# Reciprocal square roots of a hybrid encoder layer: one GpSimd power instruction in place of eleven VectorE instructions

## The chip, the cores and the metric

The kernel runs on one core of a Trainium2 chip. The metric is the device time in microseconds (us) of one execution. Before the change it is 2738.26 us, the median of three runs (2738.12 to 2742.08). Engines are called by the profile's names: PE (TensorE matmuls), PEld (its weight loads), DVE (VectorE), ACT (ScalarE), POOL (GpSimd) and SP (SyncE, which here issues every DMA).

## What is computed

One layer of an encoder in float32, 2048 tokens by 1024 features:

```
h = rmsnorm(x, norm_mix_w);  proj = h @ w_in
q, k, v, z, xbc, dt_raw, qx = split(proj)
q = partial_rope(rmsnorm(q, q_norm_w));  k = partial_rope(rmsnorm(k, k_norm_w))
attn_out = windowed_gqa(q, k, v, attn_sink)
ssd_out  = bidirectional_ssd(z, xbc, dt_raw, ...)        # its output is gated and rmsnormed in two groups
xatt_out = memory_cross_attention(qx, mem, ...)          # rmsnorm of mem, of its keys and of the queries
x = x + concat(attn_out, ssd_out, xatt_out) @ w_out
x = x + square(relu(rmsnorm(x, norm_mlp_w) @ w_mlp_up)) @ w_mlp_down

rmsnorm(t, w) = t * rsqrt(mean(t * t) + 1e-6) * w
```

Seven norms occur. Each needs, per token (and per head or group), one reciprocal square root: a column of 128 tokens by 2 to 16 numbers at a time.

## The kernel before

Tokens go in tiles of 128, and a tile's tokens lie on the 128 partitions wherever a norm's factors are made. Matmuls in float32 are done as three products of float32r parts: a value is split into a high part (ACT rounds it) and a low part (DVE or POOL subtracts). The program has three stages.

Stage 1 goes over the upper half of the sequence (1024 tokens), then over the lower half. For each half it makes the k, v and dt projection for eight tiles (`kv_products`), the factors of the input norm for the eight tiles at once (`x_stats`, L803), then normalises and rotates k in two groups of four tiles (`kvdt_tiles`, L901, which calls `head_norm`, L666, and `rope`, L691), convolves twelve column blocks (`xbc_col`, L818), and makes the memory queries in pairs of tiles (`xattn_pair`, L1019) and the attention queries in pairs of tiles (`q_pair`, L997). The upper half also makes the memory's keys and values (`mem_kv`, L711). Stage 2 runs the window attention and the state-space part for 16 chunks. Stage 3 makes the output projection for eight pairs of tiles (`out_pair`, L1400) and, one step later, the norm ahead of the MLP (`mid`, L1482); then come the two matmuls of the MLP, in a form with seven block products in place of eight.

Every reciprocal square root is made by `rsqrt` (L497). It is called 40 times: twice in `x_stats` (8 numbers per token), twice in `mem_kv` (2 and 8), four times for k (8), eight times in `xattn_pair` (8), eight times in `q_pair` (16), eight times in `out_pair` (4) and eight times in `mid` (2). Before the change each call is eleven VectorE instructions on at most 128x16 numbers: an integer guess, a scaling, and three Newton steps of three instructions, each of which needs the one before it.

What follows k's factors matters below. In `head_norm` (L666) ACT squares the products scaled by the input norm's factor `r`, DVE sums the squares and adds the epsilon, `rsqrt` follows, DVE multiplies its result by `r` (L673), and POOL multiplies k by that (L677). Then `rope` takes four POOL instructions for each tile (L698 to L701), and PE transposes the tile (`kvdt_tiles`, L919). POOL also makes the low parts of the weights of `xbc_col` (the splits `W<-Z,W`, L481).

The order of the instructions isn't the order in which the code calls them. A recorder (`Program`, L74) collects all of them with their dependences; `plan` (L287) then runs a list schedule over them with a cost in ns for each (`cost`, L176) and a latency between engines (`LAT`, L80), and takes the earliest instruction in program order that is ready on an engine. `schedule` (L399) issues them in that order. So one changed cost moves instructions everywhere behind it, on all engines, and the DMAs on SP with them; each engine then works its own list strictly in order. All of the program's instructions are issued from L414 (L416 after the change), so that tiles, not lines, tell them apart: `small` holds the factors and other small columns, `B` the normalised k and q and the convolution's buffers, `E` the parts of `rope`, `W` and `X` the split weights and inputs of stage 1, `Z` loaded weights, `bank` is PSUM, and `const` holds r (`self.r1`), the identity and the cosines.

Of the kernel before, what the change touches and what calls it, by code (L numbers as in the profile page):

```python
# [10 lines left out]
F32 = mybir.dt.float32  # L11
F32R = mybir.dt.float32r
I32 = mybir.dt.int32
AF = mybir.ActivationFunctionType
ALU = mybir.AluOpType
# [4 lines left out]
P = 128  # L20
# [15 lines left out]
NCOL, NROW = sum(n for _, n in COLS), sum(n for _, n in ROWS)  # L36
# [37 lines left out]
class Program:  # L74
# [101 lines left out]
    def cost(self, eng, name, args, kw, aps):  # L176

        n = max(self.free(args[0] if args else kw["out"]), 1)
        isap = lambda x: isinstance(x, (View, bass.AP))
        if eng == "PE":  # L180
            if name == "transpose":
                return 109
            return 108 if n < 32 else n / 2.4 + 13 if args[1].dtype == F32R and n >= 256 else n * 4 / 2.4 + 6
        if eng == "ACT":
            n_ap = sum(isap(kw.get(k)) for k in ("bias", "scale", "accum_out"))
            return 93 * n_ap + 0.834 * n + (50 if isinstance(args[1], View) and args[1].psum else 93)
        if eng == "DVE":
            if name == "reciprocal":
                return 69 + 6.25 * n
            n = max([n] + [self.free(a) for a in aps])  # L190
            if name == "memset":
                return 9 + 1.04 * n
            ap_scalar = any(isap(x) and self.free(x) == 1 for x in args[2:4]) and "scalar" in name
            fast = name in ("tensor_copy", "tensor_scalar") and not any(isinstance(a, View) and a.psum for a in aps)
            return 69 + (0.52 if fast else 1.041) * n + (61 if ap_scalar else 0)
        if eng == "POOL":
            bcast = any(d[0] == 0 and d[1] > 1 for a in aps[1:] for d in a.ap.ap[1:])
            return 148 + (1.667 if bcast else 2.1) * n if name == "tensor_tensor" else 40 + 1.6 * n
        return 475

# [260 lines left out]
class Hybrid:  # L461
# [34 lines left out]

    def rsqrt(self, pool, v, n):  # L497

        nc = self.nc
        y = pool.tile([P, 32], F32, "nr_y")[:, :n]  # L500
        h = pool.tile([P, 32], F32, "nr_h")[:, :n]
        t = pool.tile([P, 32], F32, "nr_t")[:, :n]
        nc.vector.tensor_scalar(y.bitcast(I32), v.bitcast(I32), -0.5, 1597463007.0, ALU.mult, ALU.add)
        nc.vector.tensor_scalar(h, v, -0.5, None, ALU.mult)
        for _ in range(3):
            nc.vector.tensor_tensor(t, y, y, ALU.mult)
            nc.vector.tensor_tensor(t, t, h, ALU.mult)
            nc.vector.scalar_tensor_tensor(y, t, 1.5, y, ALU.add, ALU.mult)
        return y

    def ps(self):
# [2 lines left out]

    def constants(self):
        nc, a = self.nc, self.a
        sizes = dict(ident=128, ones=128, eps=1, cols=NCOL, r1=16)
        self.mem.use("const", F32, **{"c_" + k: (n, 1) for k, n in sizes.items()})
        sizes = dict(triU=128, triL=128, amask=768, rows=NROW, dt=512, acs=512, wst=512, dec=512, edge=48, negA=32, nsk=8)
        self.mem.use("late", F32, **{"c_" + k: (n, 1) for k, n in sizes.items()})  # L520

        def c(name, shape):
            return self.mem.tile([P] + shape, F32, "c_" + name)

        self.eps = c("eps", [1])
        nc.vector.memset(self.eps, EPS)
        nc.scalar.activation(self.eps, self.eps, AF.Copy)
        self.ident = c("ident", [P])
        make_identity(nc, self.ident)
        self.ones = c("ones", [P])  # L530
        nc.gpsimd.memset(self.ones, 1.0)
        self.triU = c("triU", [P])
        self.triL = c("triL", [P])
        for t, sgn in ((self.triU, 1), (self.triL, -1)):
            nc.gpsimd.affine_select(out=t, in_=self.ones, compare_op=ALU.is_ge, fill=0.0, base=0,
                                    pattern=[[sgn, P]], channel_multiplier=-sgn)
        self.mask = c("amask", [6 * P])
        nc.gpsimd.memset(self.mask, 0.0)
        for o, sgn in ((0, 1), (2, -1), (3, 1), (5, 1)):
            m = self.mask[:, o * P:(o + 1) * P]  # L540
            nc.gpsimd.affine_select(out=m, in_=m, compare_op=ALU.is_ge, fill=NEG, base=0,
                                    pattern=[[sgn, P]], channel_multiplier=-sgn)

        cols, rows = c("cols", [NCOL]), c("rows", [NROW])
        first = NCOL - 256
        self.load(cols[:, :first], a["cols"][:, :first])

        def cut(t, table, name, shape=None):
            at = sum(n for k, n in table[:[k for k, _ in table].index(name)])
            v = t[:, at:at + dict(table)[name]]  # L550
            return v.rearrange("p (a b) -> p a b", a=shape[0]) if shape else v

        self.w_mix, self.w_mem, self.w_mlp, self.w_ssd, self.cb, self.sd = (
            cut(cols, COLS, n) for n in ("w_mix", "w_mem", "w_mlp", "w_ssd", "cb", "sd"))
        self.cw, self.cos, self.sin = cut(cols, COLS, "cw", (NXC,)), cut(cols, COLS, "cos", (NJ,)), cut(cols, COLS, "sin", (NJ,))
        for v in (cut(cols, COLS, "cw"), self.cb):
            nc.vector.tensor_scalar(v, v, 0.5, None, ALU.mult)
        self.qw, self.kw, self.xqw, self.xkw, self.sink, self.dtb, self.al = (
            cut(rows, ROWS, n) for n in ("qw", "kw", "xqw", "xkw", "sink", "dtb", "al"))
        self.r1 = c("r1", [NJ])  # L560
        self.dt = c("dt", [NJ, 32])
        self.acs = c("acs", [NJ, 32])
        self.wst = c("wst", [NJ, 32])
        self.dec = c("dec", [NJ, 32])
        self.edge = c("edge", [NXC, 4])
        self.negA = c("negA", [32])
        self.nsk = c("nsk", [8])
        yield
        self.load(cols[:, first:], a["cols"][:, first:])
        self.load(rows, a["rows"].rearrange("(o n) -> o n", o=1).broadcast_to([P, NROW]))  # L570
        nc.vector.tensor_scalar(self.qw, self.qw, 0.125, None, ALU.mult)
        nc.vector.tensor_tensor(self.xkw, self.xkw, self.xqw, ALU.mult)
        nc.scalar.activation(self.negA, self.al, AF.Exp)
        nc.vector.tensor_scalar(self.negA, self.negA, -1.0, None, ALU.mult)
        nc.vector.tensor_scalar(self.nsk, self.sink, -1.0, None, ALU.mult)
        yield

    def memory(self):
        m = self.mem
        m.use("small", F32, nr_y=(32, 3), nr_h=(32, 3), nr_t=(32, 3), nr_v=(32, 3), xmx=(32, 2), xsm=(32, 2),  # L580
              amx=(32, 3), ang=(32, 3), asm=(32, 3), aes=(32, 3), rm=(32, 1), s2=(32, 2))

    def memory1(self):
# [1181 lines left out]
```

## Time and profile before

| what | value |
|---|---|
| time, median of three runs | 2738.26 us (2738.12 to 2742.08) |
| span of the profiled execution, first to last instruction | 2734.9 us |
| PE busy | 2706.3 us, 99% of the span |
| DVE busy | 1900.8 us, 70%, 3102 instructions |
| ACT busy | 1331.6 us, 49% |
| POOL busy | 554.2 us, 20%, 488 instructions |
| mean granted TensorE clock | 0.997 |

The profile gives the profiled execution's span, which is 3.4 us under the median of the three runs; a start and an end outside the first and last instruction lie around it. Times in the profile are counted from the span's start. A row of a timeline gives start, duration, engine, operation, tiles and shape (rows with xN are N instructions in a row on that engine), and in brackets the idle time of the engine ahead of it with what ended it. `PEclk` is the clock that TensorE was granted, in tenths (or as a share, in the view by windows).

### The profile page before, as it was taken

To read this page: it belongs to the slowest core of one execution; us is meant where nothing else is said; L and a number is where in the kernel's file an instruction comes from. 1 tells how busy PE (TensorE), PEld (TensorE's weight loads), DVE (VectorE), ACT (ScalarE), POOL (GpSimd) and SP (SyncE) were. 2 spreads that over 40 slices of the span, in tenths; PEclk is the share of its full clock that TensorE was granted. 3 is DMA by queue.
4 is the path that set the end of the run, shared out by engine and by line. 5 is a ranking of instruction groups with operands and counts; after the bars stand their busy time and mean duration, and the time that the engine had idled before them with its cause. 6 is when DMAs were issued, how large, how long until landed. Compare 5 with 4: busy or idle time off the path is not lost.

```text
span 2734.9 us, 37074 instructions
## 1 busy us (share of the span) xinstructions
PE 2706.3 (99%) x13486; PEld 2236.3 (82%) x13486; DVE 1900.8 (70%) x3102; ACT 1331.6 (49%) x2229; POOL 554.2 (20%) x488
## 2 busy tenths in 40 slices
PE   8999999999999999999999999999999999999999
PEld 7788887787778888788888888888888888888887
DVE  6884689956677686776666785857757584857666
ACT  6545534353567676733333543535353443535352
POOL 3203444455445554410101000000000000000000
PEclk9999999999999999999999999999999999999999
DMA  6651446545877786865555954536272745435241
GB/s 239 213 182 59 133 147 190 172 158 177 268 251 235 214 257 205 271 204 200 193 192 202 342 195 146 170 102 214 80 259 93 253 162 169 154 119 197 90 165 62
DMA packets 264886, 501.40 MB, mean 183 GB/s; under 512 B 26096, under 2 KB 99072, under 8 KB 264704
## 3 DMA queue, kind: packets, MB, share of 16 engines
q1 hardware_dynamic: 264704, 499.04, 55.3%
q8 instruction: 106, 1.74, 0.3%
q14 instruction: 76, 0.62, 0.1%
HBM read 381.51 MB, written 117.45 MB: 182 GB/s over the span
## 4 chain that ended last, share of the span: by engine, by line
PE 92%; DVE 2%; POOL 2%; ACT 1%; issue 1%; DMA 1%; SPq 0%; DVEq 0%; ACTq 0%; POOLq 0%
PE bank L414 92%; POOL B L414 1%; DVE B L414 1%; DVE A L414 1%; POOL E L414 1%; DVE small L414 0%; DMA Z<-in_w_out_dram 0%; ACT C L414 0%; SPq L414 0%; DMA W<-erow_d 0%; DVE W L414 0%; ACT A L414 0%; ACT B L414 0%; POOL W L414 0%; DVE X L414 0%
## 5 line engine op out<-in xcount | busy, mean ns | idle before, releaser
L414 PE MATMUL bank<-X,late 128*128 128x512 f32 x1792 | 552.3, 389 | 0.0
L414 PE MATMUL bank<-A,E 128*128 128x512 f32 (+2 forms) x1152 | 404.8, 380 | 1.1 <-ACT A L414 0.7
L414 PE MATMUL bank<-X,A 128*128 128x512 f32 (+1 forms) x1264 | 396.1, 390 | 0.2 <-DMA A<-v_d 0.2
L414 PEld LDWEIGHTS bank<-X,late 128*128 128x128 f32 x1792 | 336.3, 188 | 69.6
L414 PE MATMUL bank<-late,C 128*128 128x512 f32 x896 | 348.6, 389 | 0.0
L414 PE MATMUL bank<-late,E 128*128 128x512 f32 x896 | 348.6, 389 | 0.0
L414 PE MATMUL bank<-W,X 128*128 128x512 f32 (+1 forms) x1536 | 339.4, 373 | 6.5 <-ACT W L414 5.8
L414 PE MATMUL bank<-X,W 128*128 128x512 f32 x1344 | 324.3, 398 | 0.7 <-ACT E L414 0.6
L414 PE MATMUL bank<-X,X 128*128 128x512 f32 x1216 | 317.6, 401 | 0.6 <-DVE X L414 0.6
L414 PEld LDWEIGHTS bank<-W,X 128*128 128x128 f32 x1536 | 265.8, 190 | 51.5 <-ACT W L414 5.8
L414 PEld LDWEIGHTS bank<-X,W 128*128 128x128 f32 x1344 | 250.8, 189 | 55.8 <-issue 3.4
L414 PEld LDWEIGHTS bank<-X,X 128*128 128x128 f32 x1216 | 225.2, 188 | 56.0 <-issue 8.9
L414 PEld LDWEIGHTS bank<-A,E 128*128 128x128 f32 x1152 | 211.7, 188 | 43.0 <-issue 2.8
L414 PEld LDWEIGHTS bank<-X,A 128*128 128x128 f32 (+1 forms) x1264 | 192.5, 173 | 50.5 <-issue 3.5
L414 DVE TENSOR_TENSOR A<-Z,late 128x1024 fp32r<-128x1024 f32 x100 | 121.9, 1221 | 149.0 <-ACT late L414 142.6
L414 DVE TENSOR_TENSOR B<-B,bank 128x512 f32<-128x512 f32 x286 | 189.7, 680 | 33.3 <-PE bank L414 32.6
L414 PEld LDWEIGHTS bank<-late,E 128*128 128x128 f32 x896 | 168.2, 188 | 34.9
L414 PEld LDWEIGHTS bank<-late,C 128*128 128x128 f32 x896 | 168.2, 188 | 34.8
L414 ACT CAST late<-Z 128x1024 fp32r<-128x1024 f32 x100 | 105.1, 1051 | 140.0 <-PE bank L414 101.3
L414 ACT ACTIVATE C<-C,small 128x384 f32<-128x384 f32 (+1 forms) x256 | 143.8, 598 | 36.0 <-DVE small L414 35.9
L414 ACT ACTIVATE W<-W 128x512 f32<-128x512 f32 x224 | 134.4, 627 | 48.9 <-DVE W L414 45.9
L414 DVE SCALAR_TENSOR_TENSOR B<-B,const 128x1022 f32<-128x1022 f32 (+1 forms) x96 | 146.0, 1524 | 3.9 <-ACT B L414 3.0
(178 smaller groups left out, 4259.3 us busy)
## 6 DMA issues: line engine op xcount, KB each, us to landing
X<-xc_d SPq DMA_DIRECT2D x112, 1024.0 KB
xc_d<-E SPq DMA_DIRECT2D x56, 512.0 KB
Z<-in_w_z_dram SPq DMA_DIRECT2D x32, 512.0 KB
W<-erow_d SPq DMA_DIRECT2D x64, 256.0 KB
X<-in_w_up_dram SPq DMA_DIRECT2D x32, 512.0 KB
A<-in_w_up_dram SPq DMA_DIRECT2D x32, 512.0 KB
X<-in_w_down_dram SPq DMA_DIRECT2D x32, 512.0 KB
A<-in_w_down_dram SPq DMA_DIRECT2D x32, 512.0 KB
```

What stands on the lines that cost most here:

```text
L414: o.fn(*[fix(x) for x in o.args], **{k: fix(x) for k, x in o.kw.items()})
```

## The change

`rsqrt` becomes one POOL instruction, `tensor_tensor` with the operation power: the variance to the power of a tile that holds -0.5. That tile, `root`, is filled once at the start. The planner gets a cost for such an instruction, 500 ns and 40 ns for each number of a row, so 820 ns for 8 numbers. The buffers of the Newton steps fall away.

```diff
@@ cost
             bcast = any(d[0] == 0 and d[1] > 1 for a in aps[1:] for d in a.ap.ap[1:])
+            if ALU.pow in args:
+                return 500 + 40 * n
             return 148 + (1.667 if bcast else 2.1) * n if name == "tensor_tensor" else 40 + 1.6 * n
@@ rsqrt
-        nc = self.nc
         y = pool.tile([P, 32], F32, "nr_y")[:, :n]
-        h = pool.tile([P, 32], F32, "nr_h")[:, :n]
-        t = pool.tile([P, 32], F32, "nr_t")[:, :n]
-        nc.vector.tensor_scalar(y.bitcast(I32), v.bitcast(I32), -0.5, 1597463007.0, ALU.mult, ALU.add)
-        nc.vector.tensor_scalar(h, v, -0.5, None, ALU.mult)
-        for _ in range(3):
-            nc.vector.tensor_tensor(t, y, y, ALU.mult)
-            nc.vector.tensor_tensor(t, t, h, ALU.mult)
-            nc.vector.scalar_tensor_tensor(y, t, 1.5, y, ALU.add, ALU.mult)
+        self.nc.gpsimd.tensor_tensor(y, v, self.root[:, :n], ALU.pow)
         return y
@@ constants
-        sizes = dict(ident=128, ones=128, eps=1, cols=NCOL, r1=16)
+        sizes = dict(ident=128, ones=128, eps=1, root=32, cols=NCOL, r1=16)
...
+        self.root = c("root", [32])
+        nc.gpsimd.memset(self.root, -0.5)
@@ memory
-        m.use("small", F32, nr_y=(32, 3), nr_h=(32, 3), nr_t=(32, 3), nr_v=(32, 3), xmx=(32, 2), xsm=(32, 2),
+        m.use("small", F32, nr_y=(32, 3), nr_v=(32, 3), xmx=(32, 2), xsm=(32, 2),
```

The planner writes another order for every engine. Three lists at one place, the first normalised k (`kvdt_tiles` for the first four tiles of the upper half, soon after the start), show how. On VectorE, before, from the sum of k's squares on (`TENSOR_REDUCE small`); `late<-E` is the sum of dt and its bias, `B 128x256` belongs to `dt_half`:

```order
L414 TENSOR_REDUCE small_87<-B_101 128x8
L414 TENSOR_SCALAR small_87<-small_87 128x8 x3
L414 TENSOR_TENSOR late_89<-E_103,late_89 128x32
L414 TENSOR_TENSOR small_87<-small_87 128x8
L414 TENSOR_TENSOR late_89<-E_103,late_89 128x32 x2
L414 TENSOR_TENSOR small_87<-small_87 128x8
L414 TENSOR_TENSOR late_89<-E_103,late_89 128x32
L414 SCALAR_TENSOR_TENSOR small_87<-small_87 128x8
L414 TENSOR_TENSOR small_87<-small_87 128x8 x2
L414 SCALAR_TENSOR_TENSOR small_87<-small_87 128x8
L414 TENSOR_TENSOR small_87<-small_87 128x8
L414 TENSOR_SCALAR B_101<-B_101 128x256
```

The same place on VectorE after the change; `small_87<-small_87,const_88` is the product of the factors with r (L673 before):

```order
L416 TENSOR_REDUCE small_87<-B_101 128x8
L416 TENSOR_SCALAR small_87<-small_87 128x8
L416 TENSOR_TENSOR small_87<-small_87,const_88 128x8
L416 TENSOR_TENSOR late_89<-E_103,late_89 128x32 x4
L416 TENSOR_TENSOR B_101<-bank_77,Z_102 128x512
```

The Newton instructions are gone, and the product with r stands right behind the epsilon. On GpSimd, before, from the weight splits on; `B_101<-B_101,small_87` multiplies k by its factors, and the rows with `E_103` are `rope`:

```order
L414 TENSOR_TENSOR W_0_98<-Z_102,W_0_97 128x1024 x4
L414 TENSOR_TENSOR B_101<-B_101,small_87 128x512
L414 TENSOR_TENSOR E_103<-B_101,const_88 128x32 x2
L414 TENSOR_TENSOR B_101<-E_103 128x2x8
L414 TENSOR_TENSOR E_103<-B_101,const_88 128x32
L414 TENSOR_TENSOR B_101<-E_103 128x2x8
```

And after, where `small_87<-const_88` is the power of `x_stats` and `small_87<-small_87,const_88` the power for k:

```order
L416 TENSOR_TENSOR W_0_98<-Z_102,W_0_97 128x1024
L416 TENSOR_TENSOR small_87<-const_88 128x8
L416 TENSOR_TENSOR small_87<-small_87,const_88 128x8
L416 TENSOR_TENSOR W_0_98<-Z_102,W_0_97 128x1024 x2
L416 TENSOR_TENSOR B_101<-B_101,small_87 128x512
L416 TENSOR_TENSOR E_103<-B_101,const_88 128x32 x3
L416 TENSOR_TENSOR B_101<-E_103 128x2x8
```

Two splits now stand behind the power for k and ahead of the product with k, and one split (of four) has gone behind the rotations. On PE, before, around the first transpose of a k tile (`const_88,B_101`; the others are products of `xbc_col`):

```order
L414 MATMUL bank_77<-X_0_93,W_0_98 128x512
L414 MATMUL bank_80<-X_0_93,W_0_98 128x512
L414 MATMUL bank_77<-X_0_93,W_0_97 128x512
L414 MATMUL bank_78<-const_88,B_101 128x128
L414 MATMUL bank_77<-X_0_94,W_0_97 128x512
```

And after the change:

```order
L416 MATMUL bank_79<-X_0_94,W_0_97 128x512
L416 MATMUL bank_77<-const_88,B_101 128x128
L416 MATMUL bank_79<-X_0_93,W_0_98 128x512
L416 MATMUL bank_79<-X_0_93,W_0_97 128x512
L416 MATMUL bank_77<-const_88,B_101 128x128
```

Before, 55 products of `xbc_col` stand between the last product of `kv_products` and this transpose; after the change 26 do, and the four transposes of the group stand within 13 places, where before they were spread over 47. The transpose of r by `x_stats` (`bank<-const 8x128`) has moved seven products forward. The four k groups, the query pairs and stages 2 and 3 are reordered too; the number of PE instructions is the same.

## The prediction

> **What bounds the kernel now.** I read the page first: busy times and the granted clock in 40 slices.
>
> ```profile
> span 2734.9 us, 37074 instructions
> PE 2706.3 (99%) x13486; PEld 2236.3 (82%) x13486; DVE 1900.8 (70%) x3102; ACT 1331.6 (49%) x2229; POOL 554.2 (20%) x488
> PEclk9999999999999999999999999999999999999999
> ```
>
> PE is busy for 2706.3 of 2734.9 us, so it is the bound, and 28.6 us is all that lies between its instructions. VectorE, which the change relieves, is at 70%. Next I looked at where PE idles, by stretches, and then at who ends its waits (columns: us in total, times, longest).
>
> ```profile
> 1175.00:1525.00 350.00, 350.00 (x1628) 291.48 (x1627) 230.32 (x489) 124.62 (x193) 40.78 (x56) 1.00 0.59 207
> 1525.00:2735.00 1210.00, 1206.33 (x5329) 998.91 (x5327) 812.84 (x850) 539.26 (x686) 0.00 (x0) 1.00 0.48 161
> ```
>
> The first row is the output projection, where 16 of the 40 square roots are: PE has no idle time there at all. The second is the MLP, without square roots; its 3.7 us of idle is the end of the program. So whatever the change can bring must come from stages 1 and 2.
>
> ```profile
> PE bank L414 <- POOL B L414: 8.1, 7, 3.3
> PE bank L414 <- ACT W L414: 5.8, 1, 5.8
> ```
>
> The second is the start of the program (the first weights). The first is the one that matters: POOL's tile `B` is a normalised and rotated k or q that PE is to transpose, so behind each of these seven waits stands a square root. I then went to each. The two long ones are the first two groups of k, A and B below; these are PE's rows there.
>
> ```profile
> 45.36 12.67 PE L414 MATMUL bank<-X,W 128*128 128x512 f32 x55
> 61.38 0.33 PE L414 MATMUL bank<-const,B 128*128 128x128 f32 x1 [3.35 <-POOL B L414]
> ...
> 85.72 6.86 PE L414 MATMUL bank<-X,W 128*128 128x512 f32 x29
> 94.71 0.33 PE L414 MATMUL bank<-const,B 128*128 128x128 f32 x1 [2.13 <-POOL B L414]
> ```
>
> A costs 3.35 us of waiting and B 2.13 us. Each has a second price, which the windows show (PE busy and count, granted clock, DMA share, GB/s):
>
> ```profile
> 62.00:65.40 3.40, 3.40 (x9) 0.50 0.00 0
> 65.40:80.00 14.60, 14.60 (x70) 1.00 0.57 158
> 96.00:99.50 3.50, 3.50 (x13) 0.52 0.48 150
> 731.00:737.80 6.80, 5.98 (x32) 0.50 0.98 315
> ```
>
> Behind each of these two waits the clock is granted at half for 3.4 us, which takes up to 1.7 us more of PE's time. A is thus worth 5.05 us and B 3.83 us. (The third dip, at 731 us, is at the start of stage 2, where no square root is.) The other waits for square roots are small: from 320 to 362 us, the first of the lower half, and from 660 to 685 us, the last queries.
>
> ```profile
> PE bank L414 <- POOL B L414: 1.1, 2, 0.8
> PE bank L414 <- ACT E L414: 0.6, 1, 0.6
> PE bank L414 <- DVE A L414: 0.3, 1, 0.3
> ...
> PE bank L414 <- POOL B L414: 1.5, 3, 0.7
> ```
>
> That is C, 2.0 us, and D, 1.5 us. All that a perfect square root could give back is 5.05 + 3.83 + 2.0 + 1.5 = 12.4 us, 0.45% of the time. A measurement of this kernel can tell about 0.2%, 5.5 us, from no change.
>
> **What is removed.** 40 calls of eleven instructions are 440: 240 products, 120 fused ones, 80 with a scalar. Their groups (count | busy, mean ns):
>
> ```profile
> L414 DVE TENSOR_TENSOR small<-small 128x8 f32<-128x8 f32 (+3 forms) x273 | 61.3, 224 | 15.5 <-ACT C L414 10.2 <-ACT small L414 0.3
> L414 DVE SCALAR_TENSOR_TENSOR small<-small 128x2 f32<-128x2 f32 (+3 forms) x152 | 36.3, 242 | 3.6
> L414 DVE TENSOR_SCALAR small<-small 128x8 f32<-128x8 f32 (+7 forms) x106 | 21.6, 235 | 5.4 <-ACT B L414 4.3
> ```
>
> 240 x 0.224 + 120 x 0.242 + 80 x 0.235 = 102 us of VectorE. On the time that is worth nothing by itself: VectorE isn't the bound, and PE's work hides it. What counts is the latency of a call where PE waits, and how the new order uses it.
>
> **What is added.** 40 power instructions on POOL. The trace of before has none, so I bound one by POOL's shortest and longest group with two inputs:
>
> ```profile
> L414 POOL TENSOR_TENSOR B<-E 128x16 f32<-128x16 f32 x32 | 10.4, 339 | 0.5
> L414 POOL TENSOR_TENSOR W<-Z,W 128x1024 fp32r<-128x1024 f32 x38 | 96.0, 2530 | 204.1 <-ACT W L414 201.9 <-PE bank L414 2.2
> ```
>
> It is not below 0.34 us, the price of a 128x16 subtraction, and I take 2.53 us as the other end. A power of 2 to 16 numbers is nearer to the small row; I take the planner's own 0.82 us for 8 numbers, which lies in between and by which the order was made. For all 40 that is about 33 us of POOL, which is at 20%. A rule of the Trainium skill speaks against the move: GPSIMD Engine Reference, section 4.1, calls GpSimd the wrong engine for elementwise work, about twice as slow as VectorE for two inputs. The rows agree (339 ns for a small POOL instruction, 224 ns for a small one of VectorE, its stalls included). By that rule alone a power would cost 0.34 us instead of 0.82, and A below would be 0.5 us better; but eleven instructions become one, so the rule doesn't turn the sign.
>
> **A, worked out.** The rows of before: PE, VectorE, ACT, POOL:
>
> ```profile
> 43.79 0.96 PE L414 MATMUL bank<-W,X 128*128 128x288 f32 x6
> 44.59 0.27 PE L414 MATMUL bank<-const 128*8 128x128 f32 x1
> ...
> 37.06 0.17 DVE L414 TENSOR_SCALAR const<-const 128x8 f32<-128x8 f32 x1
> ...
> 39.27 0.17 DVE L414 COPY const<-small 128x8 f32<-128x8 f32 x1
> ...
> 48.39 2.65 DVE L414 TENSOR_SCALAR small<-small 128x8 f32<-128x8 f32 x3
> ...
> 56.76 0.16 DVE L414 TENSOR_TENSOR small<-small,const 128x8 f32<-128x8 f32 x1
> ...
> 45.15 0.24 ACT L414 COPY E<-bank 8x128 f32<-8x128 f32 x1
> ...
> 46.27 1.27 ACT L414 ACTIVATE B<-C,const 128x128 f32<-128x128 f32 x4
> ...
> 48.55 2.39 POOL L414 TENSOR_TENSOR W<-Z,W 128x1024 fp32r<-128x1024 f32 x1 [1.15 <-ACT W L414]
> ...
> 56.99 1.07 POOL L414 TENSOR_TENSOR B<-B,small 128x512 f32<-128x512 f32 x1 [1.07 <-DVE small L414]
> 58.14 1.51 POOL L414 TENSOR_TENSOR E<-B,const 128x32 f32<-128x32 f32 x2
> ```
>
> For `x_stats`, v is there at 37.23. Eleven instructions end at about 39.25; a power ends at about 38.2. That 1 us is hidden: ACT's next rows need PE's transpose of r, which stands seven products (0.96 / 6 = 0.16 us each) further forward and so comes at about 43.5 instead of 44.6. A power here has some 5 us of cover. From it, ACT squares k at 44.6 to 45.9 instead of 46.3 to 47.5 (a split's rounding no longer stands ahead of it), VectorE's sum and epsilon end at about 46.9, and POOL's power at 47.9. Before, it took from 48.4 to the product with r at 56.76: the Newton steps stood in VectorE's line between long instructions, and the first three rows, 2.65 us, stood still while POOL ran the split at 48.55. So the factors of k are ready 8 us earlier, at 48.1. But the new order spends that. Behind the power POOL has two splits of 2.4 us, so the product with k starts at about 52.7, only 4.3 us earlier than 56.99. From there to PE it took 61.38 - 56.99 = 4.4 us, with stalls (the two rotations at 58.14 took 1.51 us). Six rotation steps now stand ahead of the first transpose instead of five: 1.07 + 6 x 0.36 = 3.2 us without stalls, 4.7 with the same ones; so it can run between 56.0 and 57.4. And PE reaches it after 26 products instead of 55, 26 x 0.230 = 6.0 us after 45.36, at 51.4. PE then waits 4.6 to 6.0 us, where it waited 3.35, and the next three transposes, now close behind, cost up to 1 us more. With a half clock of about 1 to 1.7 us I put A at 7.0 us instead of 5.05: **+2.0 us**, between -5.0 (the wait vanishes) and +6.
>
> **B.** The second group's chain, in the trace of before:
>
> ```profile
> 89.59 1.04 POOL L414 TENSOR_TENSOR B<-B,small 128x512 f32<-128x512 f32 x1 [12.21 <-DVE small L414]
> ```
>
> POOL stood idle for 12.2 us until VectorE's Newton steps, spread among the convolution's long instructions, were through. With a power the factors come about 10 us or more earlier against PE's list, and PE's first transpose of this group stands some 74 places earlier (17 us). On POOL its power stands behind A's rotations (done at about 61) and two splits of 2.4 us, so it runs at about 67, and with the product and the first rotations its tiles come at 73 to 80. PE gets there at about 78: 57 for A, 81 products at 0.23 and some 2 us for transposes and half a clock. The wait and its half clock should all but go: **-3.8 us**, between that and +2. By the Trainium skill (TensorE: Matmul & The Clock Gate, section "HAM oscillation"), only idle of over some 3.4 us costs clock; by that rule B would be worth only its 2.1 us and the sum below 1.7 us worse. The row at 96 us says otherwise: half a clock behind 2.13 us of idle. I go by the row.
>
> **C and D.** At C the Newton steps of `x_stats` are on PE's path, and a power with two hops between engines should save 1 to 2 us of it, of which I count **-1.0 us** (between -2 and +1). At D a power of 16 numbers (1.1 us by the planner) goes into POOL's own line ahead of the product with q, and takes there what VectorE gives: **0**, between -1.5 and +2. Stages 2 and 3 are only reordered: **0**, and since the start of stage 2 has waits and a half clock of its own (the row at 731 us), plus or minus 4 us.
>
> Sum: 2.0 - 3.8 - 1.0 = -2.8 us. The span goes from 2734.9 to 2732.1, and the median, 3.4 us above it, from 2738.3 to **2735.5 us**.
>
> **The rivals.** *The waits only trade places* (B's gain eaten by A and by the new order): 2738.3, the same for a measurement. For it speaks that the planner reckons both chains as nearly in time already, and was wrong by 2 to 3 us at both places; the same error would stand in the new order. *All four places clear*: 2738.3 - 12.4 = 2725.9 at most, faster. For it speaks that factors come 8 us earlier at A; against it, the two splits ahead of the product with k. *The power instruction is slow*: slower. It is on the path at A, B and three of the k and q groups of C and D, so about 5 x (price - 0.82 us) is added; that passes the bound of 0.2% (2743.7) at a price of 2.5 us, and at 3.8 us the time is 2735.5 + 14.9 = 2750.4. For it speaks that VectorE needs eleven steps for what POOL is to do in one; against it, that POOL's rows for small tiles lie at 0.34 us. In stage 3 even 4 us would be hidden, since PE has 350 us there without a wait.
>
> **Chances.** The forecast 0.45; the traded places 0.15; both lie within 0.2% (2732.8 to 2743.7), so the same: 0.60. All or most places clear: 0.22, faster. A slow power: 0.18, slower. The range goes from 2727 (nearly all of the clear places) to 2747 (a power of 3.1 us); about 0.15 is left outside.
>
> **What would show it.** Right: a power row of 0.6 to 1.2 us; VectorE down by about 100 us of busy time with the span unmoved; PE idle at the first k group near 51 us, longer than 3.35 us; no wait at the second; stage 3 without idle as before. Wrong: a power above 2.5 us, or PE idle at several query pairs (slow power), or no wait at the first group (clear places), or a change of more than 4 us in stage 2, which would mean that the new order, not the square root, decides.

## The result and the profile after

The changed kernel takes 2782.98 us (median of four runs, 2781.12 to 2785.29); the kernel before, beside it, 2738.24 us. The ratio is 1.0158, with a 95% interval of 1.0144 to 1.0172: 44.7 us slower, where the prediction had 2735.5 us and a range of 2727 to 2747. The page of the kernel after, its span and busy times:

```profile
span 2782.3 us, 36644 instructions
PE 2717.7 (98%) x13486; PEld 2241.6 (81%) x13486; DVE 1842.8 (66%) x2662; ACT 1334.3 (48%) x2229; POOL 621.4 (22%) x529
```

VectorE has lost its 440 instructions and 58.0 us (0.13 us each, or 0.17 in `e9_last` below, where the order is held; not the 0.23 of the prediction's groups), GpSimd has gained 67.2 us, and the span is 47.4 us longer (the profiled execution of before ends 3.4 us below its median, that of after 0.7). TensorE's work is the same; it waits longer, and it is 11.4 us longer busy at it, since the clock is at half more often: its mean is 0.993, before 0.997. The stages say where. A row has the stretch and its length, then busy time and count of PE, PEld, DVE, ACT and POOL, the clock, the DMA share and GB/s. Rows 1 and 2 are 280 us to the start of stage 2, and stage 2, of before; rows 3 to 5 are the same two and stage 3's output projection of after.

```profile
280.00:711.60 431.60, 426.95 (x2186) 352.55 (x2185) 320.91 (x592) 189.04 (x339) 200.37 (x170) 1.00 0.52 168
711.60:1158.30 446.70, 439.75 (x2887) 352.18 (x2885) 328.29 (x779) 314.40 (x725) 235.10 (x186) 0.99 0.78 242
```

```profile
280.00:727.80 447.80, 429.12 (x2193) 352.24 (x2192) 299.62 (x418) 189.67 (x339) 239.53 (x186) 1.00 0.51 162
727.80:1202.50 474.70, 452.03 (x2902) 359.96 (x2900) 331.41 (x779) 315.71 (x725) 233.92 (x184) 0.97 0.73 225
1202.50:1636.10 433.60, 427.64 (x1968) 356.54 (x1969) 263.40 (x378) 172.78 (x263) 63.66 (x78) 0.99 0.66 227
```

At 280 us TensorE is 0.6 us behind before, by the count of its instructions, and the MLP's length agrees within 0.2 us. The rest of stage 1 is 16.2 us longer, stage 2 is 28.0 us longer, and the output projection 3.1 us (433.6 against 430.5). Stage 2 has no square root in it, so two causes are to be looked for, not one. The waits of TensorE by what ended them, in the kernel after:

```profile
PE bank L416 <- ACT X L416: 20.5, 11, 7.5
PE bank L416 <- POOL B L416: 19.8, 12, 4.1
```

`POOL B`, the normalised k and q, went from 8.1 us to 19.8; `ACT X`, TensorE's inputs that ScalarE splits, was 2.0 us in all and is now 20.5: 15.0 of them in stage 2, which splits there the inputs of its z blocks, and 4.9 in one wait at the start of the output projection. And what a power costs, by size (count | busy, mean ns):

```profile
L416 POOL TENSOR_TENSOR small<-small,const 128x16 f32<-128x16 f32 x8 | 24.2, 3019 | 34.7 <-DVE small L416 34.7
L416 POOL TENSOR_TENSOR small<-small,const 128x8 f32<-128x8 f32 x13 | 21.5, 1651 | 46.9 <-DVE small L416 46.7
L416 POOL TENSOR_TENSOR small<-small,const 128x4 f32<-128x4 f32 x8 | 9.1, 1142 | 13.5 <-DVE small L416 13.5
L416 POOL TENSOR_TENSOR small<-small,const 128x2 f32<-128x2 f32 x9 | 8.1, 901 | 179.0 <-DVE small L416 179.0
```

The shortest of each size took 2.90, 1.64, 1.02 and 0.71 us, which is 390 ns and 157 ns for each number of a row. The planner booked 500 + 40n: 1.14 us for 16 numbers and 0.82 us for 8. The prediction took that price over.

### The profile page after: what moved, and what is told of

It reads as the page before. It is cut to its first block, busy times and chain, and to the rows that moved or that the text cites. A ratio compares the mean times of both kernels' runs of the same rounds, so it can differ in the third digit from the quotient of the medians.

```text
span 2782.3 us, 36644 instructions
## 1 busy us (share of the span) xinstructions
PE 2717.7 (98%) x13486; PEld 2241.6 (81%) x13486; DVE 1842.8 (66%) x2662; ACT 1334.3 (48%) x2229; POOL 621.4 (22%) x529
## 4 chain that ended last, share of the span: by engine, by line
PE 69%; ACT 2%; DMA 1%; DVE 1%; issue 1%; POOL 0%; SPq 0%; DVEq 0%; ACTq 0%
PE bank L416 69%; ACT C L416 1%; DMA W<-erow_d 1%; DVE X L416 0%; ACT X L416 0%; DMA Z<-in_w_z_dram 0%; DMA B<-in_x_dram 0%; DMA Z<-in_xT_dram 0%; DVE small L416 0%; DVE A L416 0%; ACT A L416 0%; DVE W L416 0%; DMA Z<-in_w_out_dram 0%; DVE C L416 0%; SPq L416 0%
## 5 line engine op out<-in xcount | busy, mean ns | idle before, releaser
L416 PE MATMUL bank<-X,X 128*128 128x512 f32 x1216 | 323.7, 407 | 16.2 <-ACT X L416 15.8
L416 DVE SCALAR_TENSOR_TENSOR B<-B,const 128x1022 f32<-128x1022 f32 (+1 forms) x96 | 151.8, 1588 | 3.4 <-ACT B L416 2.5
```

The lines of the kernel that those rows point to most:

```text
L416: o.fn(*[fix(x) for x in o.args], **{k: fix(x) for k, x in o.kw.items()})
```

## The experiments

Two theories were set against each other: P, the price (powers longer than booked make TensorE wait), and L, the list (the planner, fed other costs, finds another order, which in stage 2 happens to be worse). In the texts on record "lists" and "orders" are the engines' instruction orders. "Stage 1's rest" below is the time from 280 us to the start of stage 2, so that what a kernel lost ahead of 280 us is in it too.

**The price booked right** (`e1_booked`), the changed kernel with one line edited:

```diff
-                return 500 + 40 * n
+                return 390 + 157 * n
```

> The change, with the planner's cost of a power set to what the profile after shows (390 + 157 n ns: 1.65 us for 8 numbers, 2.9 for 16, instead of 0.82 and 1.14). Theory P (the loss comes from a power that takes two to three times what the planner booked, so that engines wait at the places where it stands and later): with the right cost the lists fit again and the time comes back to 2738 to 2746 us. Theory L (the loss of stage 2, some 31 of 47 us, is chance: any new list there may be good or bad): another list, so anywhere between 2740 and 2780 us, with waits in stage 2 that have nothing to do with a power.

2758.81 us, ratio 1.0073 (1.0058 to 1.0088). Stage 1's rest falls from 447.8 to 434.1 us; stage 2 still takes 467.1 us. TensorE's waits for `POOL B` in stage 1's rest are gone, though a power of 16 still takes 2.90 us: its place now leaves it the time. So, as far as one new order can show it, the wrong booking cost stage 1 most of its 16 us, and the larger part of the loss isn't touched by it.

**The new order without the power** (`e2_cheap`): the same order on every engine, but the 24 powers of stage 1 are subtractions of the same tiles, booked as before, so that this kernel leaves those square roots out; the 16 of stage 3 stay powers.

```diff
-    def rsqrt(self, pool, v, n):
+    def rsqrt(self, pool, v, n, op=ALU.subtract):
...
-        self.nc.gpsimd.tensor_tensor(y, v, self.root[:, :n], ALU.pow)
...
+        self.nc.gpsimd.tensor_tensor(y, v, self.root[:, :n], op)
...
```

> The lists of the changed kernel on all engines, instruction for instruction, but the 24 powers of stage 1 replaced by subtractions of the same size (the factors of those norms are then wrong numbers; the 16 of stage 3 stay powers). It separates price from list. Theory P: 0.3 to 0.4 us instead of 1.6 to 2.9, the 16 us of stage 1 vanish and with them what follows in stage 2: 2732 to 2742 us. Theory L: the 16 us of stage 1 vanish, the 31 us of stage 2 stay, since its list is the same: 2764 to 2770 us.

2766.71 us, ratio 1.0100 (1.0085 to 1.0115). Stage 1's rest and stage 2 of this kernel:

```profile
280.00:709.30 429.30, 424.05 (x2170) 350.15 (x2168) 289.49 (x416) 186.87 (x335) 204.14 (x186) 1.00 0.52 168
709.30:1184.50 475.20, 453.05 (x2900) 361.31 (x2899) 330.63 (x779) 315.65 (x725) 233.97 (x184) 0.97 0.74 226
```

Stage 1's rest is well (429.3 us), and stage 2 is as bad as with the power (475.2). In this order the power's price is thus worth 2782.98 - 2766.71 = 16.3 us, and the order 28.5 us.

**Only stage 3** (`e3_stage3`): the power in `out_pair` and `mid`, Newton steps elsewhere, so that the order of stages 1 and 2 stays.

> Powers in stage 3 alone (8 of 4 numbers, 8 of 2), Newton steps elsewhere; the lists of stages 1 and 2 are those of before. Both theories: PE has no idle time in stage 3, so 2738 us, within 2 us either way. If it is over 2741, stage 3 is not as covered as the profile says.

2737.86 us, ratio 1.0000 (0.9990 to 1.0009): these 16 powers, of 0.82 and 1.02 us on average, cost and bring nothing.

**A re-planning with no other change** (`e4_replan`), the kernel before with 1 ns added to the planner's cost of a VectorE instruction:

```diff
-            return 69 + (0.52 if fast else 1.041) * n + (61 if ap_scalar else 0)
+            return 70 + (0.52 if fast else 1.041) * n + (61 if ap_scalar else 0)
```

> The kernel before, with 1 ns added to the planner's cost of most VectorE instructions: no instruction is added, removed or slower on the chip, but the lists come out differently from the middle of stage 1 on. It measures what a new list alone is worth. Theory P: 2738 us within 4 us. Theory L: off by 10 us or more, as the 31 us of stage 2 would be of that kind.

2745.08 us, ratio 1.0023 (1.0014 to 1.0033), between the numbers of both theories. One nanosecond in a table of costs is worth 6.9 us. They lie neither in stage 1's rest (430.4 us) nor in stage 2 as it is measured here (448.2): the new order puts some 48 of stage 2's TensorE instructions behind the first of the output projection, which takes 438.5 us. Both stages together take 886.7 us, before 877.2.

**The old order with the power** (`e5_held`), the other half of the crossing. The planner still plans eleven VectorE instructions; when the program is written out, one power stands at the place of the first of them.

```diff
             for _, i in order:
                 o = ops[i]
+                if i in self.newton:
+                    if self.newton[i]:
...
+                        self.tc.nc.gpsimd.tensor_tensor(y, v, root, ALU.pow)
+                    continue
...
+            nc.newton.update(dict.fromkeys(range(at, at + 11)))
+            nc.newton[at] = (y, v, self.root[:, :n], self.root)
```

> The order of every engine is the one of the kernel before, since the planner still plans eleven VectorE instructions; only when the program is written out does one GpSimd power stand at the place of the first of them. Theory P (the power itself is too dear where its result is awaited): the q pairs still wait for their 2.9 us powers and the k groups for their 1.64 us, so 10 to 20 us of stage 1 stay lost and the time is 2748 to 2760 us. Theory L (the new order that the planner found loses most of it): stage 2 takes 445 to 449 us as before and not 475, the VectorE is 60 us less busy, and the time is 2732 to 2744 us.

2750.60 us, ratio 1.0046 (1.0030 to 1.0063). Stage 1's rest and stage 2:

```profile
280.00:723.90 443.90, 429.63 (x2180) 353.84 (x2178) 291.23 (x416) 188.69 (x338) 236.32 (x186) 0.99 0.52 163
723.90:1172.60 448.70, 440.57 (x2886) 352.24 (x2885) 328.27 (x779) 314.41 (x725) 234.95 (x186) 0.99 0.78 240
```

Stage 2 is as before but for 2 us: with `e2_cheap`, the order alone decides there. In stage 1's rest 12.3 us remain; there P holds. Where they come from stands in GpSimd's own list, at the first attention-query pair of the upper half, and in TensorE's wait for it:

```profile
312.29 1.30 POOL L423 TENSOR_TENSOR E<-B,const 128x128 f32<-128x128 f32 x3
314.30 3.33 POOL L421 TENSOR_TENSOR small<-small,const 128x16 f32<-128x16 f32 x1 [0.71 <-DVE small L423]
317.60 0.31 POOL L423 TENSOR_TENSOR B<-E 128x64 f32<-128x64 f32 x1
...
318.65 1.11 PE L423 MATMUL bank<-const,B 128*128 128x128 f32 x4 [2.57 <-POOL B L423]
```

The power of the *next* pair stands in the middle of the running pair's rotation: GpSimd waits 0.71 us for its input, computes for 3.33 us, and only then finishes the `B<-E` that TensorE's transposes need. The 2.57 us of waiting are that.

**Each power twice** (`e6_held2`), a second copy of the issuing line:

```diff
                         self.tc.nc.gpsimd.tensor_tensor(y, v, root, ALU.pow)
+                        self.tc.nc.gpsimd.tensor_tensor(y, v, root, ALU.pow)
```

> As the kernel with held orders, but each power is issued twice in a row (the second overwrites the same result), which adds 1.64 us to each of the eight-column groups and 2.9 us to each of sixteen columns. Theory P: the time rises by at least 10 us over the held kernel with one power, as every power is awaited. Theory L: with these orders most powers have slack, and it rises by 0 to 8 us, all of it before 750 us of the span, by less than the sum of the added powers, some 70 us.

2784.27 us, ratio 1.0171 (1.0155 to 1.0186): 33.7 us more than with one, 32.5 of them in stage 1's rest, none in stage 2. L's 0 to 8 us were far off: at this place of the held orders the powers have little slack.

**The place in the queue** (`e9_last`): as `e5_held`, with the power at the place of the last of the eleven.

```diff
-            nc.newton[at] = (y, v, self.root[:, :n], self.root)
+            nc.newton[at + 10] = (y, v, self.root[:, :n], self.root)
```

> Orders held as in the kernel before, but the power stands at the place of the last of the eleven VectorE instructions, no longer at that of the first, so that GpSimd finishes the rotary work of the running head pair before it starts the next pair's power. Theory Q (the 12.8 us of the held kernel are GpSimd's queue: a power of 2.9 to 3.3 us stands in front of work that TensorE waits for): the waits of 2.57 us at 316, 330 and 677 us shrink below 1 us and the time is 2734 to 2742 us. Theory D (the power's own duration is too long wherever it stands, as its result is awaited): the stretch between 280 us and stage 2 stays 440 us or longer and the time is 2746 us or more.

2739.73 us, ratio 1.0001 (0.9992 to 1.0010): the same as before, as Q had it. The same place on GpSimd:

```profile
312.74 1.29 POOL L423 TENSOR_TENSOR E<-B,const 128x128 f32<-128x128 f32 x3
313.99 0.76 POOL L423 TENSOR_TENSOR B<-E 128x64 f32<-128x64 f32 x1
...
316.43 2.90 POOL L421 TENSOR_TENSOR small<-small,const 128x16 f32<-128x16 f32 x1
321.71 1.90 POOL L423 TENSOR_TENSOR B<-B,small 128x1024 f32<-128x1024 f32 x1 [2.38 <-DVE small L423]
```

The rotation runs through, the power follows, and its result is still there 2.38 us before GpSimd gets the product that uses it. TensorE's waits for `POOL B` in stage 1's rest, of before, after, `e5_held` and this kernel (us in total, times, longest):

```profile
PE bank L414 <- POOL B L414: 2.6, 5, 0.8
```

```profile
PE bank L416 <- POOL B L416: 15.8, 11, 3.1
```

```profile
PE bank L423 <- POOL B L423: 11.7, 7, 2.6
```

```profile
PE bank L423 <- POOL B L423: 2.4, 2, 1.8
```

So with the order of before the power isn't too slow for its place in the chain; it is too long a block to stand in front of other work of GpSimd. (In the order of the kernel after it is otherwise, as the part on why the prediction was wrong shows.) Newton steps are eleven blocks of 0.17 us, between which VectorE's other work fits. VectorE's rows of before at this stretch's first pair, the first three small instructions behind the sum of squares and the product of the finished factors with r:

```profile
306.23 0.46 DVE L414 TENSOR_SCALAR small<-small 128x16 f32<-128x16 f32 x3
...
310.86 0.17 DVE L414 TENSOR_TENSOR small<-small,const 128x16 f32<-128x16 f32 x1
```

Spread like that they took 4.6 us, longer than a power, and TensorE waited for `POOL B` 0.3 us in all from 290 to 350 us.

**Only the groups of eight columns** (`e10_konly`), `e5_held` with `if n == 8` ahead of the replacement. (The text on record names the groups wrongly: eight columns are `x_stats`, `mem_kv`'s keys, k, and the memory queries, 15 of the 40 calls. The output projection has four.)

> Orders held, and only the groups of eight columns (the key groups and the two of the out projection) take the power, at the place of the first; the query pairs of sixteen columns and all others keep the eleven VectorE instructions. If the loss lies in the query pairs alone: 2733 to 2739 us, with the stretch from 280 us to stage 2 at 430 to 433 us. If the key groups cost too: above 2741 us.

2741.72 us, ratio 1.0010 (1.0001 to 1.0018), just above the second number, with an interval that reaches below it: 2.6 us are lost, with a wait of 2.25 us at 353 us, where the power of `x_stats` (1.65 us) stands in front of an attention-query pair's rotation. If the parts add up, about 10 of the 12.8 us are the attention-query pairs' and the rest is due to the others.

**A factor at almost no cost** (`e11_free`), which leaves the square roots of 8 and 16 columns out, 23 of the 40:

```diff
-                        self.tc.nc.gpsimd.tensor_tensor(y, v, root, ALU.pow)
+                        self.tc.nc.vector.tensor_scalar(y, v, 0.5, None, ALU.add)
...
-        if True:
+        if n > 4:
             nc.newton.update(dict.fromkeys(range(at, at + 11)))
```

> Orders held, and the eleven VectorE instructions of every group of eight or sixteen columns become one VectorE addition of 0.5 (a wrong factor, not a square root), with nothing given to GpSimd: what a square root at almost no cost would bring. If the VectorE's Newton steps are on no path but at the two places A and B: 2728 to 2737 us, at most 10 us below the kernel before. If the VectorE is what holds TensorE in stage 1: 2725 us or less. If the freed VectorE only moves the waits: 2736 to 2740 us.

2735.03 us, ratio 0.9985 (0.9976 to 0.9994). With the order held, these square roots at almost no cost are worth 4.1 us, not 12.4. At the first two k groups TensorE still waits 3.04 and 1.83 us (before: 3.35 and 2.13), so with this order the Newton steps made 0.3 us of each wait. The rest must come from what else stands in the lists there, which no run took apart.

**Four instructions of stage 2 moved** (`e12_early`): the changed kernel, where its longest wait is 7.47 us for `ACT X`, around whose end the clock is at half for 6.8 us (the second row is a window of 6.9 us).

```profile
784.22 6.04 PE L416 MATMUL bank<-X,X 128*128 128x512 f32 x15 [7.47 <-ACT X L416]
```

```profile
781.30:788.20 6.90, 3.98 (x9) 3.04 (x10) 1.45 (x3) 3.35 (x6) 0.00 (x0) 0.51 0.23 80
```

On ScalarE the two splits that end this wait stand behind eight instructions of the softmax, which had waited for VectorE. The edit marks them and the two that end the 2.40 us at 751 us, and when the program is written out they are moved forward by so many places of ScalarE's list:

```diff
+            if b == 1 and k in (0, 1, 4, 5):
+                nc.early.append((len(nc.ops), 10 if k < 2 else 8))
...
```

> The changed kernel with every order as it was but for four ScalarE instructions early in stage 2: the splits X<-Z of the first z block, whose products TensorE waited for (2.40 us at 751 us, 7.48 us at 777 us), stand ten and eight instructions further ahead, before the softmax exponentials that stood in front of them. If the order on ScalarE makes these waits: the 7.5 us wait falls to 4 us or less and the 2.4 us one below 1 us, stage 2 is 5 to 12 us shorter than the changed kernel's 474.6 us, and the time is 2770 to 2778 us. If the transfers of Z (or VectorE, late with the maxima) make them: the waits stay, or move behind the exponentials, and the time is 2779 to 2787 us.

2785.40 us, ratio 1.0174 (1.0160 to 1.0188): no gain, as its text has it for waits that the transfers or VectorE make, and stage 2 takes 475.7 us. The trace of this kernel, ScalarE at the first pair and TensorE there and at the second:

```profile
749.39 0.72 ACT L427 ACTIVATE X<-Z,const 128x512 fp32r<-128x512 f32 x1 [2.24 <-DMA Z<-in_xT_dram]
...
752.53 1.67 PE L427 MATMUL bank<-const,C 128*128 128x128 f32 x4 [2.69 <-ACT C L427]
...
784.13 0.73 PE L427 MATMUL bank<-X,X 128*128 128x512 f32 x2 [2.96 <-ACT X L427]
787.68 2.93 PE L427 MATMUL bank<-X,X 128*128 128x512 f32 x6 [2.81 <-DVE X L427]
```

The 7.47 us became 2.96 + 2.81, but the first pair now waited 2.24 us for its transfer with the softmax behind it, and TensorE waited 2.69 us for that instead. The account of these waits by four instructions of ScalarE falls: mending one place moved the wait to the next transfer and the next engine.

**Is it the power's order, or any new one?** Six more orders. Each is a kernel told above with 1 to 3 ns put on or taken off the same cost of a VectorE instruction (69), as in `e4_replan`: before (`e7_replan2`, `e13_n68`, `e14_n72`), after (`e8_after1`), or `e1_booked` (`e15_p68`, `e16_p70`).

> The kernel before, with 2 ns added to the planner's cost of each VectorE instruction, and no other edit: the same work in another order. Theory L: the time is anywhere from 2730 to 2765 us, off the kernel before by more than 4 us, and most of the difference lies in stage 2. Theory P, by which the order as such costs nothing: 2734 to 2742 us.

> The changed kernel, with 1 ns added to the planner's cost of each VectorE instruction. Theory L: stage 2 and the start of stage 3 move by 10 us or more against the changed kernel's, while stage 1 keeps its 16 us, since the power is still booked too short: 2745 to 2775 us. Theory P: 2779 to 2787 us as the changed kernel.

> The kernel before, with 1 ns taken from the planner's cost of each VectorE instruction: a further order with Newton steps. Theory S (planning with the power as such brings worse orders in stage 2): stage 2 takes 445 to 461 us, as in the three orders with Newton steps so far, 2735 to 2754 us in all. Theory C (any re-planning draws a stage 2 between 445 and 480 us by chance): as likely as not it takes 462 us or more.

> The kernel before, with 3 ns added to the planner's cost of each VectorE instruction. Theory S: stage 2 takes 445 to 461 us. Theory C: as likely as not 462 us or more.

> The changed kernel with the power booked at its measured time, 390 + 157 n ns, and 1 ns taken from the planner's cost of each VectorE instruction: a further order with the power. Theory S: stage 2 takes 465 us or more, as in the three orders with the power so far, and the time is 2755 us or more. Theory C: as likely as not stage 2 takes less than 462 us and the time is below 2750 us.

> The changed kernel with the power booked at 390 + 157 n ns, and 1 ns added to the planner's cost of each VectorE instruction. Theory S: stage 2 takes 465 us or more. Theory C: as likely as not less than 462 us.

All orders side by side, stages in us by the first TensorE instruction of each. The ratios to before of the six, in the order of their texts: 1.0053 (1.0038 to 1.0068), 1.0144 (1.0129 to 1.0159), 1.0088 (1.0058 to 1.0117), 1.0099 (1.0070 to 1.0128), 1.0099 (1.0070 to 1.0129) and 1.0099 (1.0069 to 1.0128).

| planned with | VectorE cost | time, us | stage 1's rest | stage 2 |
|---|---|---|---|---|
| Newton steps (before) | 69 | 2738.2 | 431.6 | 446.6 |
| Newton (`e4_replan`) | 70 | 2745.1 | 430.4 | 448.2 |
| Newton (`e7_replan2`) | 71 | 2753.3 | 431.4 | 460.9 |
| Newton (`e14_n72`) | 72 | 2765.0 | 428.7 | 477.5 |
| Newton (`e13_n68`) | 68 | 2761.9 | 438.7 | 464.7 |
| power at 390 + 157n (`e1_booked`) | 69 | 2758.8 | 434.1 | 467.1 |
| power at 390 + 157n (`e15_p68`) | 68 | 2765.1 | 431.8 | 470.5 |
| power at 390 + 157n (`e16_p70`) | 70 | 2764.9 | 435.4 | 465.8 |
| power at 500 + 40n (after) | 69 | 2783.0 | 447.8 | 474.6 |
| power at 500 + 40n (`e8_after1`) | 70 | 2777.1 | 444.6 | 470.6 |

Stage 2 of `e14_n72`, which has no power anywhere:

```profile
708.70:1186.20 477.50, 452.64 (x2887) 359.10 (x2886) 329.55 (x779) 315.70 (x725) 232.30 (x186) 0.96 0.73 227
```

It is as long as the changed kernel's or longer. So theory S (orders with the power are worse as such) falls in its plain form, on `e13_n68` and `e14_n72`; `e15_p68` and `e16_p70` came out as it had said. The four re-plannings of the kernel before draw a stage 2 between 448 (which is too good, as told above) and 478 us, those with a power one between 466 and 475, and the order of the kernel before is the best of the ten. The five drawn with a power have a mean of 469.7 us and the four re-planned without one 462.8; with a scatter of 30 us, that difference stays open. `e7_replan2`, `e13_n68` and `e14_n72` are off the kernel before by 15 to 27 us, far beyond what P allowed; `e8_after1` moved by 6 us only, more than P and less than L expected. In stage 1's rest the price shows again: 431.8 to 435.4 us with the power booked right, hardly other than the Newton steps' 428.7 to 438.7, and 444.6 and 447.8 us booked short.

## Why the prediction was wrong

**The step that failed** is "Stages 2 and 3 are only reordered: 0 [...] plus or minus 4 us". It measured +28.0 and +3.1 us. The crossing of `e2_cheap` and `e5_held` shows the cause: the new order with a cheap stand-in has it (475.2 us), the old order with the power hasn't (448.7 us), and 1 to 3 ns of cost bring orders from 448 to 478 us. The prediction's sum had no term for a new draw of the order and its range no room for one, though it said that each changed cost moves instructions on all engines, and named a change in stage 2 as what would show that the order decides. Why a drawn stage 2 is long is shown only as far as its waits, for ScalarE's splits in the main; its cause stays open. That mending its longest wait alone gains nothing is what `e12_early` showed.

**The price.** 0.82 us was the planner's number, not a row's. It measured 1.64 us for 8 numbers and 2.90 for 16, just beyond the 2.53 us of the bound. The rival of the slow power had the right sign, but it multiplied by five places on the path and came to 5 x 0.82 = 4 us for 1.64; the measured loss is 16.3 us in this order: TensorE waits 15.8 us for `POOL B` at eleven places of stage 1's rest, where C and D were given -1.0 and 0. (C was misread besides: of its 2.0 us, the 1.1 for `POOL B` are waits for attention-query pairs of the upper half, at 327.71 and 354.46 us, and only 0.9 are at `x_stats`.) Both signs that it had named came: a power above 2.5 us, and TensorE idle at several query pairs. At four of the six longest of these waits the power stands in the chain itself, with GpSimd idle ahead of it. GpSimd's and TensorE's rows at the upper half's first attention-query pair, of after:

```profile
303.21 2.90 POOL L416 TENSOR_TENSOR small<-small,const 128x16 f32<-128x16 f32 x1 [5.17 <-DVE small L416]
306.46 1.91 POOL L416 TENSOR_TENSOR B<-B,small 128x1024 f32<-128x1024 f32 x1 [0.35 <-DVE small L416]
...
311.64 0.66 PE L416 MATMUL bank<-const,B 128*128 128x128 f32 x4 [2.82 <-POOL B L416]
```

The planner had placed TensorE's transposes for a power of 1.14 us, 1.76 us less than it takes; with the price booked right these waits are gone (`e1_booked`). GpSimd's queue is what counts in the order of before (`e5_held`, `e9_last`). By the rule of the Trainium skill that the prediction weighed (GPSIMD Engine Reference, section 4.1, elementwise work with two inputs is about twice as slow on GpSimd), the sign was right. Its answer, that one instruction replaces eleven, failed for 16 numbers: 11 x 0.17 us of VectorE's shortest rows is 1.9 us, and the one takes 2.90. In all it held, though not by much: in `e9_last` GpSimd gains 63.0 us and VectorE loses 72.7.

**A** was right in its mechanism. TensorE's and GpSimd's rows of after:

```profile
55.39 0.47 PE L416 MATMUL bank<-const,B 128*128 128x128 f32 x1 [4.06 <-POOL B L416]
...
46.62 1.64 POOL L416 TENSOR_TENSOR small<-small,const 128x8 f32<-128x8 f32 x1 [5.65 <-DVE small L416]
48.23 4.74 POOL L416 TENSOR_TENSOR W<-Z,W 128x1024 fp32r<-128x1024 f32 x2
52.92 1.10 POOL L416 TENSOR_TENSOR B<-B,small 128x512 f32<-128x512 f32 x1
```

TensorE went idle at 51.33 us (51.4 predicted), for 4.06 us (4.6 to 6.0), and the product with k began at 52.92 (52.7): factors earlier, two splits in front, a longer wait. The half clock lasted 6.8 us where up to 3.4 had been counted, 1.0 of them still in the wait (the window below is 6.9 us long):

```profile
54.30:61.20 6.90, 5.81 (x16) 4.43 (x17) 6.76 (x13) 5.04 (x12) 3.01 (x16) 0.51 0.22 75
```

5.81 us of work at half the clock cost some 2.9 us, so A came to 4.06 + 2.9 = 7.0 us, as predicted. That the sum agrees so well is luck: the wait was shorter and the half clock longer than worked out.

**B** was right: the wait and its half clock went. GpSimd's last rotation of the second group ended at 81.6 us, about as early as worked out, and TensorE transposed the group without a wait, the first tile among the eight transposes at 77.00 and the last at 84.06. TensorE's and VectorE's rows of after:

```profile
77.00 1.03 PE L416 MATMUL bank<-const,B 128*128 128x128 f32 x8
...
84.06 0.27 PE L416 MATMUL bank<-const,B 128*128 128x128 f32 x1
...
93.55 0.42 DVE L416 TENSOR_TENSOR B<-bank,late 128x256 f32<-128x256 f32 x1 [2.27 <-ACT late L416]
...
96.04 0.52 PE L416 MATMUL bank<-const,B 128*128 128x128 f32 x3 [2.38 <-DVE B L416]
```

The wait at 96.04 is another one: these are the transposes of `dt_half`, whose inputs VectorE copies just before, and VectorE had itself stood idle for 2.27 us until ScalarE was through. So the square root's wait went, and a new one came 12 us later, at work without a square root, as the rival of the traded places had it. Taken together the first 280 us became 0.6 us longer, where A and B had summed to -1.8: there TensorE's waits for `POOL B` fell by 1.4 us, those for VectorE's `B` rose by 1.8 and that for the first weights by 0.4, and the half clock took 6.8 us in both kernels.

**VectorE** lost 58 us (about 100 were foretold) and that was worth nothing, as predicted: `e9_last` has it at 1828.1 us, 72.7 less than before, in the same time. The ceiling of 12.4 us was too high, since a wait that a square root stands behind isn't made by it; `e11_free` measured 4.1 us for 23 of them. **Stage 3** covers even its own powers (`e3_stage3`).

No kernel here that computes its square roots beats the one before by more than the measurement can tell.

## What to carry to other kernels

Where a planner draws the order, measure first how far the time moves when a cost moves by a nanosecond or a few; here 1 to 3 ns moved it by 6 to 27 us, and an order that is the best of ten draws mostly loses when anything is planned anew. Judge an instruction with the order held, and take its cost from a row, since a booked price that is half the true one cost some 12 us of stage 1 here (two orders against three). One long instruction in place of eleven short ones isn't only a duration but a block in an in-order queue: look at what stands behind it there, and put it where that engine would be idle.

## What was unexpected of the hardware

- GpSimd's power on float32 takes 0.71, 1.02, 1.64 and 2.90 us for 2, 4, 8 and 16 numbers on each of 128 partitions, while a product there of 128x1024 with a column factor takes 1.91 us: about 157 ns a number against less than 2. Single powers of 16 took up to 3.35 us; what makes them longer isn't shown.
- The length of an idle stretch doesn't tell the clock's answer: in before, 2.13 us at B were followed by half a clock for 3.4 us, in after 2.38 us at 96.04 us by none, and 4.06 us at A by 6.8 us. The page TensorE: Matmul & The Clock Gate of the Trainium skill (section "HAM oscillation") has a bound of about 3.4 us of idle; the first of these rows lies below it, so the bound isn't sharp here. What decides, as far as these traces show, is where the idle time falls: in each of the 18 traces the half clocks begin on a grid of 3.413 us (in after at 54.35, 754.09, 781.39 and 1023.74 us, that is 205, 213 and 284 steps behind the first). Of the 2.13 us at B, 2.0 fall into one step of this grid, while the 2.38 us are parted into 1.65 and 0.73, and 3.09 us at 677.40 us of after, with no half clock behind them either, into 1.26 and 1.83. Behind TensorE's first instruction, a step at full clock with over 1.83 us of idle was always followed by half a clock, one with 0.97 to 1.83 us only at times.
